# A transformer layer on one core: x in four transfers with spread column sums, row factors spread by TensorE, a late modulation in small pieces, other buffers for w_out

## The chip, the cores and the metric

The kernel runs on one core of one Trainium2 chip. The metric is the device time of one execution in microseconds (us), lower is better. TensorE is called PE in the views of the profile, VectorE DVE, ScalarE ACT, GpSimd POOL, and SyncE SP; SP issues nearly all transfers. All arithmetic is in 32 bits.

## What is computed

One layer over 512 latent tokens with a context of 256 tokens, model width 1024. `w_ada` turns a condition vector into shifts, scales and gates; the first two of its six parts are needed at once, the other four (w_ada_b in the kernel) only for the output projection and the feed-forward part.

```python
mod = jax.nn.silu(c) @ w_ada[l] + b_ada[l]
sh1, sc1, g1, sh2, sc2, g2 = jnp.split(mod[:, None, :], 6, axis=-1)
a_lat = _modulate(x, norm_mix[l], sh1, sc1)       # rmsnorm * gain * (1 + scale) + shift
a_ctx = _modulate(xc, norm_mix[l], csh1, csc1)
# one projection of both by w_in: pooling input, q, k, v, o of 4 heads, two gates
#   pooling: window means over the 8 x 64 grid, a 256 x 256 product per group
#   mLSTM, 4 heads, forward and backward, chunks of 128 tokens:
S = einsum('bhtd,bhsd->bhts', qc, kc) * exp(Dm - m[..., None])
num = einsum('bhts,bhsv->bhtv', S, vc) + sa[..., None] * einsum('bhtd,bhdv->bhtv', qc, C0)
h = num / jnp.maximum(jnp.abs(den), jnp.exp(-m))[..., None]
y = sigmoid(p[5]) * pool_out + sigmoid(p[6]) * m_out
x = x + g1 * (y @ w_out)
x = x + g2 * _swiglu(_modulate(x, norm_ffn[l], sh2, sc2), w_ffn_in[l], w_ffn_out[l])
return _rmsnorm(x, norm_final)
```

## The kernel before

**Products.** Every product of two 32-bit operands is made of three matmuls on a high and a low part of each (`mm3`): high by high, high by low, low by high. Activations lie with channels on the partitions. Each weight block of 128 output channels (512 KB) comes through `wload`: SP issues its transfer into one of three buffers `wr`, ACT casts the high part (`wh`), DVE subtracts to give the low part (`wl`); both have two buffers. Other destinations are named by an argument: "wide" gives the two buffers gh and gl, ("oh", "ol") the five half-width buffers of each of these. Each engine works in program order; where the program is not ordered by hand (`manual_schedule`, used for the start and the feed-forward part's first tiles), a scheduler orders it.

**Start.** SP issues the parameters, x in eight transfers of 256 KB (one per block k of 128 channels), a tile of ones, an identity, then alternately `ada` (1 MB, one block of the first two parts of w_ada) and `wr` (w_in for six output tiles, block k). For the RMS of x, ACT squares each block, DVE adds the squares up into one tile, and PE takes column sums with a 128x2 tile of ones as the moving operand (`rstd_cols`); POOL takes the power -0.5, and PE spreads the result over the partitions (`rstd_rows`). PE multiplies zeros (`keep_warm`, tile `warm`) in between, in numbers given by `WARM`. `mod_rows` and `mod_cols` compute the shift and scale of block k, `stage` modulates block k, `products` multiplies it with six tiles of w_in.

**Heads.** For each of four heads: values, scores and applications in two halves of 256 query tokens (`scores(0)`, a filling projection tile, `apply(0)`, `scores(1)`, another tile, `turn`, `apply(1)`), then the pooling for two tiles, gates, and q and k of the next head. `decays` makes the exponential decay factors (tiles E) for a half: a row factor per query, which lies in 32 rows, is needed on all partitions. `gates` writes these 32 rows to memory (tile `rd`), and each `decays` reads its four rows back as a broadcast. POOL adds the masks, ACT takes the exponentials, DVE multiplies the scores, and the products are split into high and low parts Sp.

**Late modulation.** `late_mod` fetches 32 blocks of w_ada_b of 512 KB (tile `pb`, two buffers, shared with the pooling) and forms each product with the condition row and its sum in one DVE instruction. It is called after the keys of the next head, 11 blocks after each of heads 1 and 2, and 10 after head 3.

**Output projection.** Eight tiles of w_out; the first two run over the first six of eight input blocks, then over the other two. Tiles 2 and 3 use `wh` and `wl`, 4 and 5 gh and gl, 6 and 7 oh and ol. The feed-forward part follows.

## Time and profile before

| | before |
|---|---|
| device time, median of 3 runs | 902.11 us (901.39 to 903.74) |
| the profiled execution | 904.35 us, of which the span from first to last instruction is 902.6 us |
| PE busy | 880.6 us (98%) |
| DVE busy | 612.8 us (68%) |
| ACT busy | 434.0 us (48%) |
| POOL busy | 63.2 us (7%) |
| mean granted TensorE clock | 0.989 of 2.4 GHz |
| data moved | 121.20 MB, mean 134 GB/s |

1.75 us of the profiled execution lie outside its span. Busy shares are means over stages with different limits; matmuls are pipelined, so a busy PE is not one at its peak.

### The profile page before, as it was taken

How to read it: one execution, taken by the hardware profiler on the slowest of the kernel's cores; microseconds unless marked ns; L12 is line 12 of the kernel's file. 1: busy time of each engine (PE TensorE's matmuls, PEld its weight loads, DVE VectorE, ACT ScalarE, POOL GpSimd, SP SyncE). 2: the span in 40 equal slices, each digit the busy share in tenths (PEclk: the TensorE clock that was granted, in tenths of full speed). 3: DMA queues.
4: the chain of work that ended last, by engine and by line, in shares of the span. 5: the costliest groups of instructions: out<-in, count | busy, mean ns of one | idle time of the engine just before them, and what ended most of it. 6: DMA issues, size and time to landing. Idle time of an engine off the chain costs nothing.

```text
span 902.6 us, 14972 instructions
## 1 busy us (share of the span) xinstructions
PE 880.6 (98%) x5879; PEld 798.9 (89%) x5879; DVE 612.8 (68%) x1183; ACT 434.0 (48%) x822; POOL 63.2 (7%) x92
## 2 busy tenths in 40 slices
PE   7999999999999999999999899999999999999996
PEld 6679888899888998889988699999889998899996
DVE  3679656856599676886778658895366854867544
ACT  3455354555433552335543348574145741666442
POOL 0000010010000000001000000020011100111000
PEclk8999999999999999999999899999999999999998
DMA  9934031322067312662148750384366643766402
GB/s 338 323 105 152 9 90 33 128 83 82 24 202 253 90 51 82 220 225 82 48 152 270 245 180 29 86 216 120 94 160 147 150 117 88 204 141 129 130 1 94
DMA packets 42438, 121.20 MB, mean 134 GB/s; under 512 B 4577, under 2 KB 9345, under 8 KB 41345
## 3 DMA queue, kind: packets, MB, share of 16 engines
q1 hardware_dynamic: 36896, 110.29, 37.9%
q0 software_dynamic: 5472, 9.96, 6.7%
q8 instruction: 46, 0.75, 0.3%
q14 instruction: 24, 0.19, 0.1%
HBM read 116.55 MB, written 3.69 MB: 133 GB/s over the span
## 4 chain that ended last, share of the span: by engine, by line
PE 69%; DVE 12%; DMA 10%; issue 4%; ACT 3%; SPq 0%; POOL 0%; DVEq 0%; POOLq 0%; ACTq 0%
PE ps L181 14%; PE ps L183 14%; PE ps L182 14%; DMA pb<-in_wada_b 6%; DVE wl L152 3%; PE pat L327 3%; PE ps L540 2%; PE ps L541 2%; PE ps L539 2%; PE pat L745 2%; PE pat L743 2%; PE pat L744 2%; PE pat L182 2%; PE pat L181 2%; PE pat L183 2%
## 5 line engine op out<-in xcount | busy, mean ns | idle before, releaser
L151 ACT CAST wh<-wr 128x1024 fp32r<-128x1024 f32 (+3 forms) x80 | 80.8, 1011 | 120.7 <-PE ps L182 92.1
L181 PE MATMUL ps<-a,wh 128*128 128x512 f32 (+1 forms) x368 | 138.8, 377 | 0.0
L182 PE MATMUL ps<-a,wh 128*128 128x512 f32 (+1 forms) x368 | 138.5, 376 | 0.0
L183 PE MATMUL ps<-a,wl 128*128 128x512 f32 (+1 forms) x368 | 138.4, 376 | 0.0
L152 DVE TENSOR_TENSOR wl<-wr,wh 128x1024 fp32r<-128x1024 f32 (+3 forms) x80 | 94.2, 1179 | 36.7 <-ACT wh L151 35.6
L183 PE MATMUL ps<-act,wl 128*128 128x512 f32 (+1 forms) x216 | 78.8, 365 | 3.0 <-DVE wl L152 3.0
L183 PEld LDWEIGHTS ps<-a,wl 128*128 128x128 f32 x368 | 69.3, 188 | 12.8 <-DVE wl L152 0.2
L181 PEld LDWEIGHTS ps<-a,wh 128*128 128x128 f32 x368 | 69.3, 188 | 12.1
L182 PEld LDWEIGHTS ps<-a,wh 128*128 128x128 f32 x368 | 69.3, 188 | 11.8
L181 PE MATMUL ps<-act,wh 128*128 128x512 f32 (+1 forms) x216 | 78.4, 363 | 1.4 <-ACT wh L151 1.3
L182 PE MATMUL ps<-act,wh 128*128 128x512 f32 (+1 forms) x216 | 78.2, 362 | 0.0
L540 PE MATMUL ps<-wl,a 128*128 128x256 f32 (+1 forms) x192 | 54.4, 283 | 0.9 <-DVE wl L152 0.9
L539 PE MATMUL ps<-wh,a 128*128 128x256 f32 (+1 forms) x192 | 54.3, 283 | 0.0
L541 PE MATMUL ps<-wh,a 128*128 128x256 f32 (+1 forms) x192 | 54.2, 282 | 0.0
L972 POOL DMA_DIRECT2D ol<-in_wffi x38 | 33.4, 888 | 255.9 <-ACT ol L971 89.5
L181 PE MATMUL ps<-hp,gh 128*128 128x256 f32 x176 | 50.2, 285 | 1.0 <-ACT pat L1010 1.0
L1181 DVE SCALAR_TENSOR_TENSOR x<-ps,lb,x 128x512 f32<-128x512 f32 (+1 forms) x32 | 19.6, 616 | 45.3 <-PE ps L183 45.3
L183 PEld LDWEIGHTS ps<-act,wl 128*128 128x128 f32 x216 | 41.3, 191 | 10.2 <-DVE wl L152 4.3
L182 PE MATMUL ps<-hp,gh 128*128 128x256 f32 x176 | 49.0, 278 | 0.0
L183 PE MATMUL ps<-hp,gl 128*128 128x256 f32 x176 | 48.9, 278 | 0.0
L181 PEld LDWEIGHTS ps<-act,wh 128*128 128x128 f32 x216 | 41.4, 192 | 8.0 <-ACT wh L151 1.7
L182 PEld LDWEIGHTS ps<-act,wh 128*128 128x128 f32 x216 | 41.3, 191 | 6.5 <-DVE act L171 0.3
(309 smaller groups left out, 2541.5 us busy)
## 6 DMA issues: line engine op xcount, KB each, us to landing
wr<-in_w SPq DMA_DIRECT2D x42, 512.0 KB, 3.5
pb<-in_wada_b SPq DMA_DIRECT2D x32, 512.0 KB, 4.5
wr<-in_wffi SPq DMA_DIRECT2D x25, 512.0 KB, 4.4
ur<-in_wffi SPq DMA_DIRECT2D x19, 512.0 KB, 4.0
ol<-in_wffi POOLq DMA_DIRECT2D x38, 256.0 KB, 5.0
ada<-in_wada_a SPq DMA_DIRECT2D x8, 1024.0 KB, 8.1
wr<-in_wffo SPq DMA_DIRECT2D x16, 448.0 KB, 3.7
x<-in_xT SPq DMA_DIRECT2D x16, 256.0 KB, 6.0
```

Source lines behind the costliest of these rows:

```text
L151: nc.scalar.copy(wh, raw[:, :n])
L152: V.tensor_sub(wl, raw[:, :n], wh.bitcast(F32))
L181: nc.tensor.matmul(dst, wh, ah, start=first and i == 0, stop=False, skip_group_check=on)
L182: nc.tensor.matmul(dst, wh, al, start=False, stop=False, skip_group_check=on)
L183: nc.tensor.matmul(dst, wl, ah, start=False, stop=last and i == n - 1, skip_group_check=on)
L327: nc.tensor.matmul(acc0[i], w_first[k][i][w], aT[k][x], start=k + w + x == 0, stop=k == KT - 1 and w == 1)
L539: nc.tensor.matmul(acc[:, :n], ah, wh, start=kk == 0, stop=False)
L540: nc.tensor.matmul(acc[:, :n], ah, wl, start=False, stop=False)
L541: nc.tensor.matmul(acc[:, :n], al, wh, start=False, stop=kk == KT - 1)
L743: nc.tensor.matmul(o, sh_, vh[:, s, :], start=n == 0, stop=False)
L972: nc.gpsimd.dma_start(l, dram, accum_op=ALU.add)
L1181: V.scalar_tensor_tensor(x1[j][:, c], acc[:, c], g2[:, j:j + 1], x1[j][:, c], ALU.mult, ALU.add)
```

## The change

- x comes in four transfers of 512 KB, two blocks each; the ones are set by POOL and not fetched.
- The column sums of x are taken per pair of blocks: ACT squares one block, DVE the other and adds, and PE sums each pair at once, two sums and then a matmul of zeros. `WARM` is changed.
- In head 0, first half, the row factors are spread over the partitions by four matmuls with a broadcast column of the identity, and a DVE copy. The other seven `decays` read memory as before.
- `late_mod` hands out its blocks one or two at a time: two after the second application of head 0, and for each of heads 1 to 3 one after each of the six value tiles and two after each application.
- w_out tiles 2 and 3 go to gh and gl, 4 and 5 to oh and ol, 6 and 7 to wh and wl; the casts of 2 to 7 are held behind the last low part of y. In the feed-forward part the first pair of tiles goes to gh and gl, the second to oh and ol.

```diff
@@ -41,7 +42,7 @@
 NPAR = 168
 U0, Q0, K0, O0, G5, G6 = 0, 8, 16, 24, 32, 40
-WARM = (27, 2, 0, 1, 0)
+WARM = (16, 1, 2, 2, 5)
 NOSYNC = mybir.DependencyInfo(mybir.DependencyClass.NoSync, mybir.DependencyReason.DATA)
@@ -122,11 +123,13 @@
     V.tensor_scalar(quarter_mg, parm[:, C_MG:C_MG + KT], 0.25, None, ALU.mult)
-    x_sb = [tl("x", [P, T], F32, KT) for _ in range(KT)]
-    for k in range(KT):
-        nc.sync.dma_start(x_sb[k], xT[:, k * T:(k + 1) * T])
+    x_sb = []
+    for k in range(0, KT, 2):
+        xx = tl("x", [P, 2 * T], F32, KT // 2)
+        nc.sync.dma_start(xx, xT[:, k * T:(k + 2) * T])
+        x_sb += [xx[:, :T], xx[:, T:]]
     ones = small([P, P], "ones")
-    nc.sync.dma_start(ones, consts[:, P:2 * P])
+    nc.gpsimd.memset(ones, 1.0)
     ident = small([P, P], "ident")
@@ -190,15 +193,18 @@
+        q = None
+
         def __init__(self, urgent=()):
-            self.q = S("tmp")
             self.urgent = urgent
             self.n = {}
             self.last = {}
         def add(self, src, c):
             n = self.n[c.start] = self.n.get(c.start, 0) + 1
+            if self.q is None:
+                self.q = S("tmp")
             if n == 1:
@@ -219,6 +225,9 @@
                     nc.tensor.matmul(bank[:, 2 * i:2 * i + 2], q[:, o], ones[:, 0:2], start=t + i == 0,
                                      stop=t == len(terms) - 1, skip_group_check=True)
+            return self.power(bank, n)
+
+        def power(self, bank, n):
             sd = tl("rc", [P, 4], F32, 2)
@@ -242,9 +251,7 @@
     manual = tc.manual_schedule(engines={mybir.EngineType.PE, mybir.EngineType.Activation, mybir.EngineType.DVE})
     manual.__enter__()
-    stx = SumSq((0,))
-    for k in range(KT):
-        stx.add(x_sb[k], ALL)
+    stx = SumSq()
     rs_x = S("m")
@@ -327,8 +334,19 @@
     nf = len(FIRST)
-    sd = stx.rstd_cols(ALL)
-    keep_warm(WARM[1], warm)
+
+    bank = PS()
+    for k in range(0, KT, 2):
+        a, b = S("tmp"), S("tmp")
+        nc.scalar.activation(a, x_sb[k], AF.Square)
+        V.tensor_mul(b, x_sb[k + 1], x_sb[k + 1])
+        V.tensor_add(a, a, b)
+        for i in range(T // P):
+            nc.tensor.matmul(bank[:, 2 * i:2 * i + 2], a[:, i * P:(i + 1) * P], ones[:, 0:2], start=k + i == 0,
+                             stop=k == KT - 2, skip_group_check=True)
+            if i % 2 and k + i < KT - 2 + T // P - 1:
+                keep_warm(WARM[1], warm)
+    sd = stx.power(bank, T // P)
     rows = mod_rows(0)
@@ -491,12 +509,16 @@
             pass
-    def late_mod(lo, hi):
-        for i in range(lo, hi):
+    late = iter(range(16, 48))
+
+    def late_mod(n, behind):
+
+        for i in itertools.islice(late, n):
             wa = tl("pb", [P, PBW], F32, 2)
             nc.sync.dma_start(wa[:, :D], wada_b[i])
-            V.scalar_tensor_tensor(wa[:, :D], wa[:, :D], 0.5, crow_s, ALU.mult, ALU.mult,
-                                   accum_out=mods[:, i:i + 1])
+            with tc.issue_after(behind.ins):
+                V.scalar_tensor_tensor(wa[:, :D], wa[:, :D], 0.5, crow_s, ALU.mult, ALU.mult,
+                                       accum_out=mods[:, i:i + 1])
@@ -547,7 +569,9 @@
                     V.tensor_add(gif[:, :, d, j, :], gsrc[:, d], bsrc[:, d])
             nc.scalar.copy(vh[:, i, :DH], acc[:, :DH])
-            V.tensor_sub(vl[:, i, :DH], acc[:, :DH], vh[:, i, :DH].bitcast(F32))
+            low = V.tensor_sub(vl[:, i, :DH], acc[:, :DH], vh[:, i, :DH].bitcast(F32))
+            if h:
+                late_mod(1, low)
         return vh, vl
@@ -627,6 +651,13 @@
         rd = dram.tile([32, P], F32, name="rd")
         nc.sync.dma_start(rd, rows)
+
+        acc = PS("pat")
+        for k in range(4):
+            i = k // 2 * 16 + k % 2
+            nc.tensor.matmul(acc[:, k * P:(k + 1) * P], ident[:32, i:i + 1].broadcast_to([32, P]), rows, start=True, stop=True)
+        sa0 = S("E")
+        V.tensor_copy(sa0, acc)
         gx, c1, em = free[1:4]
@@ -645,15 +676,16 @@
                     nc.scalar.activation(wj[:, d, 0:j, :], wj[:, d, 0:j, :], AF.Exp)
                     V.tensor_scalar(wj[:, d, 0:j, :], wj[:, d, 0:j, :], 1.0 / 64.0, None, ALU.mult)
-        yield dict(g=g, gx=gx, m0=m0, c1=c1, em=em, ws=ws, rd=rd)
+        yield dict(g=g, gx=gx, m0=m0, c1=c1, em=em, ws=ws, rd=rd, sa0=sa0)
     def decays(h, gt, th):
-        sa, msk = S("E"), S("tmp")
-        nc.sync.dma_start(sa.rearrange("p (d j t) -> p d j t", d=2, j=2),
-                          gt["rd"].rearrange("(o d h j) t -> h o d j t", o=1, d=2, h=H)
-                          [h][:, :, 2 * th:2 * th + 2, :].broadcast_to([P, 2, 2, P]))
+        sa, msk = gt["sa0"] if h + th == 0 else S("E"), S("tmp")
+        if h + th:
+            nc.sync.dma_start(sa.rearrange("p (d j t) -> p d j t", d=2, j=2),
+                              gt["rd"].rearrange("(o d h j) t -> h o d j t", o=1, d=2, h=H)
+                              [h][:, :, 2 * th:2 * th + 2, :].broadcast_to([P, 2, 2, P]))
         for d, m in ((0, maskF), (1, maskB)):
@@ -760,7 +792,8 @@
             nc.gpsimd.tensor_tensor(rst[:, c2], ss[:, c2], mhalf[:, :2], ALU.pow)
             for t in range(2):
-                V.tensor_scalar(hs[t], hs[t], rst[:, 2 * th + t:2 * th + t + 1], None, ALU.mult)
+                done = V.tensor_scalar(hs[t], hs[t], rst[:, 2 * th + t:2 * th + t + 1], None, ALU.mult)
+            late_mod(2 if h or th else 0, done)
             return th, hs
@@ -842,7 +875,6 @@
         if h < H - 1:
             q_, k_ = queries(h + 1) if h else q1, keys(h + 1)
-        late_mod(16 + 11 * (h - 1), min(48, 16 + 11 * h)) if h else None
@@ -853,7 +885,9 @@
     for j in (6, 7):
-        ys[j] = tsplit(ylast[j - 6], "act")
+        ys[j] = S("act", F32R), S("act", F32R)
+        nc.scalar.copy(ys[j][0], ylast[j - 6])
+        ylow = V.tensor_sub(ys[j][1], ylast[j - 6], ys[j][0].bitcast(F32))
     close_pool("mix")
@@ -883,12 +917,15 @@
         accs.append((PS(), wload(wout[j], D)[0]))
         mm3(accs[j][0], accs[j][1][:6], ys[:6], last=False)
+    with tc.issue_after(ylow.ins):
+        w23 = [wload(wout[j], D, "wide")[0] for j in (2, 3)]
     for j, (acc, w) in enumerate(accs):
         mm3(acc, w[6:], ys[6:], first=False)
         proj_out(j, None, ALL, acc)
     for j in range(2, NW):
-        proj_out(j, wload(wout[j], D)[0], ALL)
-    wo = {j: wload(wout[j], D, "wide" if j < NW + 2 else ("oh", "ol"))[0] for j in range(NW, KT)}
+        proj_out(j, w23[j - 2], ALL)
+    with tc.issue_after(ylow.ins):
+        wo = {j: wload(wout[j], D, ("oh", "ol") if j < NW + 2 else None)[0] for j in range(NW, KT)}
@@ -1075,7 +1112,7 @@
     pw = []
     for j in range(2):
-        d = "wide" if j else None
+        d = ("oh", "ol") if j else "wide"
         pw.append((wload(wffi[2 * j], D, d)[0], wload(wffi[2 * j + 1], D, d)[0], act_tiles(j)))
```

The order in which engines meet these instructions moves at three places. First PE at the start of the program, from its first matmuls on (names: tmp_ are squares of x, summed; `ada` w_ada; rc the RMS factor). Before:

```order
L137 MATMUL pat_117<-warm 128x128 x27
L220 MATMUL ps_184<-ones,tmp_147 128x2 x4
L220 MATMUL ps_184<-ones,tmp_167 128x2 x4
L137 MATMUL pat_117<-warm 128x128 x2
L261 MATMUL ps_200<-ada_198,sil 32x256 x8
L233 MATMUL ps_211<-ident,rc_193 128x128 x4
L270 MATMUL ps_216<-ident,tmp_209 128x128 x2
L137 MATMUL pat_117<-warm 128x128
L261 MATMUL ps_238<-ada_236,sil 32x256 x8
```

With the change, from the last of x's third pair on:

```order
L345 MATMUL ps_142<-ones,tmp_165 128x2 x2
L140 MATMUL pat_109<-warm 128x128
L345 MATMUL ps_142<-ones,tmp_176 128x2 x2
L140 MATMUL pat_109<-warm 128x128
L345 MATMUL ps_142<-ones,tmp_176 128x2 x2
L268 MATMUL ps_191<-ada_189,sil 32x256 x8
L140 MATMUL pat_109<-warm 128x128 x2
L242 MATMUL ps_204<-ident,rc_186 128x128 x4
L277 MATMUL ps_209<-ident,tmp_200 128x128 x2
L140 MATMUL pat_109<-warm 128x128 x2
L268 MATMUL ps_232<-ada_230,sil 32x256 x8
L140 MATMUL pat_109<-warm 128x128 x5
```

The eight sums stood behind one block of zeros and are now in four groups, each pair of sums followed by zeros; zeros now also stand on both sides of the second `ada` group.

Second, DVE in head 1, between the scaling of the first application and the second application (Sp are low parts of decayed scores, wl a low weight part, tmp and E the factors). Before:

```order
L171 TENSOR_TENSOR Sp_2481<-tmp_2477,Sp_2480 128x512
L720 SCALAR_TENSOR_TENSOR tmp_2484<-pat_2464,g_ws,E_2327 128x256
L720 SCALAR_TENSOR_TENSOR tmp_2504<-pat_2491,g_ws,E_2327 128x256 x2
L171 TENSOR_TENSOR Sp_2488<-tmp_2484,Sp_2487 128x512
L712 SCALAR_TENSOR_TENSOR E_2332<-pat_2511,E_2332 128x256
L171 TENSOR_TENSOR Sp_2508<-tmp_2504,Sp_2507 128x512
L712 SCALAR_TENSOR_TENSOR E_2332<-pat_2511,E_2332 128x128
L712 SCALAR_TENSOR_TENSOR E_2338<-pat_2511,E_2338 128x128
L712 SCALAR_TENSOR_TENSOR E_2338<-pat_2511,E_2338 128x256
L171 TENSOR_TENSOR Sp_2527<-E_2332,Sp_2526 128x384
L171 TENSOR_TENSOR Sp_2533<-E_2338,Sp_2532 128x384
L152 TENSOR_TENSOR wl_2718<-wr_2715,wh_2717 128x1024
```

With the change:

```order
L520 SCALAR_TENSOR_TENSOR pb_2493,mods<-pb_2493,crow_s 128x1024
L520 SCALAR_TENSOR_TENSOR pb_2496,mods<-pb_2496,crow_s 128x1024
L174 TENSOR_TENSOR Sp_2516<-tmp_2512,Sp_2515 128x512
L752 SCALAR_TENSOR_TENSOR tmp_2519<-pat_2499,g_ws,E_2356 128x256
L752 SCALAR_TENSOR_TENSOR tmp_2539<-pat_2526,g_ws,E_2356 128x256 x2
L174 TENSOR_TENSOR Sp_2523<-tmp_2519,Sp_2522 128x512
L744 SCALAR_TENSOR_TENSOR E_2361<-pat_2546,E_2361 128x256
L174 TENSOR_TENSOR Sp_2543<-tmp_2539,Sp_2542 128x512
L744 SCALAR_TENSOR_TENSOR E_2361<-pat_2546,E_2361 128x128
L744 SCALAR_TENSOR_TENSOR E_2367<-pat_2546,E_2367 128x128
L744 SCALAR_TENSOR_TENSOR E_2367<-pat_2546,E_2367 128x256
L155 TENSOR_TENSOR wl_2759<-wr_2756,wh_2758 128x1024
```

Two late products now stand ahead of the first Sp of the second half, and wl, which came behind the last two Sp, now stands ahead of them.

Third, SP's queue of transfers ahead of the output projection. Before:

```order
L148 DMA wr_5306<-in_wout 128x1024
L497 DMA pb_5243<-in_wada_b 128x1024
L497 DMA pb_5246<-in_wada_b 128x1024
L148 DMA wr_5331<-in_wout 128x1024
L497 DMA pb_5249<-in_wada_b 128x1024
L148 DMA wr_5377<-in_wout 128x1024
L497 DMA pb_5252<-in_wada_b 128x1024
L497 DMA pb_5255<-in_wada_b 128x1024
L148 DMA wr_5415<-in_wout 128x1024
L497 DMA pb_5258<-in_wada_b 128x1024
L497 DMA pb_5261<-in_wada_b 128x1024
L148 DMA wr_5453<-in_wout 128x1024
```

With the change:

```order
L151 DMA wr_5310<-in_wout 128x1024
L151 DMA wr_5335<-in_wout 128x1024
L151 DMA wr_5359<-in_wout 128x1024
L151 DMA wr_5365<-in_wout 128x1024
L151 DMA wr_5458<-in_wout 128x1024
L904 DMA x_924_5293<-in_xT 128x512
```

The transfers of w_ada_b that stood between those of w_out are gone from here; they now stand in the heads.

## Rows read from the trace of the kernel before

**Rows 1.** The page's first part: busy time of each engine, its share of the span and its number of instructions.
```profile
PE 880.6 (98%) x5879; PEld 798.9 (89%) x5879; DVE 612.8 (68%) x1183; ACT 434.0 (48%) x822; POOL 63.2 (7%) x92
```

**Rows 2.** What TensorE (PE) waited for, over the whole span: waiting line, the releasing engine, tile and line, and then the us in total, the times and the longest.
```profile
PE ps L183 <- DVE wl L152: 3.0, 3, 2.1
PE ps L220 <- DVE tmp L210: 2.6, 1, 2.6
...
PE ps L181 <- ACT wh L151: 1.3, 1, 1.3
...
PE ps L327 <- ACT a L282: 1.0, 1, 1.0
PE pat L743 <- ACT Sp L170: 1.0, 1, 1.0
...
PE ps L540 <- DVE wl L152: 0.9, 1, 0.9
```

**Rows 3.** Busy time by stretch. Columns: the stretch, its length, then the busy us of each engine with its instructions, the granted TensorE clock as a share of 2.4 GHz, the DMA engines' mean busy share, GB/s. The stretches are the first 20 us; in head 0 the filling tile ahead of the first application and that application; the same two in head 2; the first 96 matmuls of the output projection, and a part of these.
```profile
0.00:20.00 20.00, 16.06 (x98) 14.37 (x99) 5.41 (x17) 7.64 (x12) 1.80 (x6) 0.83 0.89 330
118.18:124.16 5.98, 5.60 (x26) 4.35 (x25) 2.62 (x8) 3.79 (x12) 2.28 (x4) 1.00 0.42 142
124.16:133.33 9.17, 7.37 (x54) 6.76 (x55) 7.38 (x18) 6.86 (x18) 0.58 (x1) 1.00 0.20 29
314.78:320.23 5.45, 5.45 (x26) 4.51 (x25) 4.71 (x12) 3.99 (x11) 0.00 (x0) 1.00 0.40 117
320.23:326.69 6.46, 6.46 (x55) 6.45 (x54) 3.63 (x13) 3.79 (x10) 0.00 (x0) 1.00 0.37 98
493.32:522.07 28.75, 25.39 (x98) 19.76 (x96) 20.71 (x32) 11.96 (x19) 0.00 (x0) 0.88 0.81 264
515.20:521.98 6.78, 6.78 (x31) 5.58 (x30) 4.10 (x7) 3.75 (x7) 0.00 (x0) 1.00 1.01 378
```

**Rows 4.** The timeline of the first 24 us: start, length (of the whole run of instructions of one kind, with their count behind x), engine, line, operation, tiles, and in brackets the engine's idle time ahead of it and what ended that.
```profile
1.36 8.53 PE L137 MATMUL pat<-warm 128*128 128x128 f32 x54 [1.36 <-DVE warm L110]
...
9.34 3.08 DVE L210 TENSOR_TENSOR tmp<-tmp,tmp 128x512 f32<-128x512 f32 x4 [2.10 <-ACT tmp L206]
...
12.48 3.20 PE L220 MATMUL ps<-ones,tmp 128*128 128x2 f32 x16 [2.58 <-DVE tmp L210]
...
15.96 1.01 POOL L225 TENSOR_TENSOR rc<-rc,mhalf 128x4 f32<-128x4 f32 x1 [14.63 <-DVE rc L223]
...
16.67 1.94 PE L261 MATMUL ps<-ada,sil 128*32 128x256 f32 x16
...
18.53 1.72 PE L233 MATMUL ps<-ident,rc 128*128 128x128 f32 x8
...
20.09 0.38 PE L270 MATMUL ps<-ident,tmp 128*128 128x128 f32 x2
...
20.63 1.07 PE L261 MATMUL ps<-ada,sil 128*32 128x256 f32 x16
...
21.18 0.75 DVE L281 SCALAR_TENSOR_TENSOR tmp<-x,sm,ps 128x512 f32<-128x512 f32 x1
...
21.96 0.72 ACT L282 ACTIVATE a<-tmp,shm 128x512 fp32r<-128x512 f32 x1 [2.19 <-DVE tmp L281]
...
22.73 0.73 PE L327 MATMUL ps<-a,wh 128*128 128x512 f32 x2 [1.03 <-ACT a L282]
```

**Rows 5.** The chain of waits of the first 26 us, the last transfer of x: start (its issue), length, what.
```profile
4.49 6.76 DMA x<-in_xT
```

**Rows 6.** The transfers issued between 6 and 8.5 us, of them the first block of w_ada: issuing queue, count, KB each, us from issue to landing.
```profile
ada<-in_wada_a SPq DMA_DIRECT2D x1, 1024.0 KB, 7.9
```

**Rows 7.** The chain of waits between 111 and 134 us (head 0), in order of time: start, length, what.
```profile
112.39 2.07 DMA rd<-tmp
114.51 5.32 DMA E<-rd
119.99 0.75 POOL tmp L658
```

**Rows 8.** VectorE's timeline around the second application of head 1, columns as in Rows 4.
```profile
228.07 0.62 DVE L763 TENSOR_SCALAR tmp<-tmp,rst 128x256 f32<-128x256 f32 x2 [0.43 <-POOL rst L761]
...
232.78 1.09 DVE L171 TENSOR_TENSOR Sp<-E,Sp 128x384 fp32r<-128x384 f32 x2
235.15 1.23 DVE L152 TENSOR_TENSOR wl<-wr,wh 128x1024 fp32r<-128x1024 f32 x1 [1.27 <-ACT wh L151]
```

**Rows 9.** The instructions that touch the tile pb, which holds the late blocks of w_ada: duration in ns as min/median/max with the first and last start; and the transfers' us from issue to landing.
```profile
L498 DVE SCALAR_TENSOR_TENSOR pb<-pb,crow_s x32: 1205/1224/1227, 262.5 to 506.1; 128x1024 f32<-128x1024 f32 x32
...
DMA to landing us min/median/max: 3.4/4.5/5.7
```

**Rows 10.** The chain of waits between 495 and 515 us (output projection), columns as in Rows 7.
```profile
497.80 6.02 DMA wr<-in_wout
...
503.83 1.06 ACT gh L170
...
507.43 1.24 DVE wl L152
...
508.70 0.80 PE ps L183
509.50 0.43 PE ps L181
```

More of the change, by code (lines that the diff above doesn't have):

```diff
@@ L1 @@
+import itertools
 import math
```

## The prediction, made before the changed kernel ran

> **What bounds the kernel now.** I read the page's busy line first: PE is busy 880.6 of 902.6 us, the next engine, DVE, 68% [rows 1]. So PE sets the time, and a change that takes no matmul away can gain only where PE stands still, or runs at half its clock. The second view is the list of PE's waits [rows 2]. The named waits that this change can touch are 3.0 us for low weight parts (longest 2.1), 2.6 for the squares of x, 1.3 for a cast weight, 1.0 for the first modulated tile, 1.0 for a cast score product in head 0, 0.9 in the values. The reader is to see that they are few and that each belongs to one place. The third view, busy time by stretch, shows what the waits cost with their consequences [rows 3]: in the first 20 us PE is busy 16.06 at 0.83 of the clock; the filling tile and first application of head 0 take 5.98 + 9.17 us and those of head 2, with the same work, 5.45 + 6.46; the first 96 matmuls of the output projection take 28.75 us at clock 0.88, where a part of them at full clock shows 30 weight loads in 6.78 us, 0.226 us a matmul.
>
> **The start.** PE's chain to the first product at 22.73 is in the timeline [rows 4]: zeros until 9.9, 2.58 us idle for the squares, then 16 records of sums in 3.20 us, the first ada group 1.94, the spreading 1.72, transposes 0.38, after which DVE's modulation starts at 21.18 and ACT's part at 21.96. The sums, ada and the spreading ran at half clock: the second ada group at 20.63, same work at full clock, took 1.07 instead of 1.94. Now with the change. The last transfer of x landed at 4.49 + 6.76 = 11.25 [rows 5], the first ada block, issued at about 6.2, 7.9 us after issue, at 14.1 [rows 6]. The bytes in the queue ahead are the same but for the ones, so I leave both (14.0 for ada). Each pair costs DVE a square and an addition in a row, 2 x 0.77 (3.08 for four additions, [rows 4]); with the last two pairs close together the last sum tile is there at about 13.1. Its four sums with a zero matmul are ten records, about 0.1 each at full clock: 14.1. DVE's scaling and POOL's power (1.01) end at 15.4. PE meanwhile does the ada group, 14.1 to 15.2, two zero matmuls to 15.6, the spreading at full clock 0.86 to 16.5, transposes to 16.9. From the transposes' end to DVE's modulation it took 21.18 - 20.47 = 0.7, then 0.78 to ACT, then 0.77 to the product: 19.1. But five zero matmuls now stand ahead of the product, and behind the second ada group, which can't start before its block lands: 1 MB behind 0.4 MB of weights, at the 378 GB/s of the last stretch of [rows 3] 3.7 us after the first, 17.7. So 17.7 + 1.07 + ten records at 0.12 = 20.0. The gain is 22.73 - 20.0 = 2.7. Later stages hold PE longer (18 products and an ada group, 5 us and more) than their 3.7 us of transfer, so I pass the gain on whole. Bounds: if the clock falls all the same, the four groups cost 2.4 us more, gain 0.5; if x lands 2 us earlier by fewer transfers, 4.9.
>
> The Trainium skill, "DMA: Bandwidth & Descriptors", section "Rules for kernel authors", asks for transfers of at least 1 MiB, and its section "Anatomy of one DMA" fits a fixed part of about 2.0 us to each (of those that GpSimd issues; these are SP's). If the fixed parts added up, eight transfers of 256 KB would take about 21 us and four of 512 KB 13, an estimate from that page, and the start would gain some 8 us. The trace differs: all eight landed within 10.1 us of the first issue [rows 5], so the fixed parts overlap.
>
> **Head 0.** The rows of factors go to memory in 2.07 us and come back in 5.32, and only at 119.99 can POOL add masks [rows 7]; that is 7.4 us in which PE has just 4.2 us of scores and its filling tile to do. The loss is 15.15 - 11.91 = 3.2 us [rows 3]. With the change the rows reach the partitions by four matmuls and a DVE copy; POOL can start at about 114.2, and ACT's exponentials are done before the old ones began. The second half still reads memory, and its first exponential stands on ACT ahead of three casts for the first half; the transfer lands at about 119.9 as before, which leaves those casts some 3 us. The four matmuls are unseen before; by the spreading at the start, the nearest, 1.72 at half clock or 0.86 at full; by the transposes 2 x 0.38. I take 0.8. Gain 2.4, bounds 0 and 2.9.
>
> **The output projection.** The chain reads [rows 10]: a w_out transfer issued at 497.80, its cast to gh at 503.83 ahead of the next cast on ACT, DVE's low part at 507.43, PE at 508.70, and then 0.43 us a matmul for about 6 us. SP's queue shows why the loads came late: between two w_out loads stood one or two of w_ada_b, each waiting for a pb buffer that DVE had to free. With the change those blocks are spread over the heads, the w_out loads wait only for wr buffers, and tiles 2 and 3 have buffers of their own, so their parts are ready by about 500, and PE needs them from 504. The loss is 28.75 - 96 x 0.226 = 7.0 us, of which 3.4 are named waits and the rest the half clock. I take all 7.0; bound below 3.5, if another cast stalls once for 1 to 2 us and the clock falls again. In the values of head 3 the 0.9 us for late low weights [rows 2] belongs to the same queue and goes too. The moved buffers of the feed-forward part change casts from one of 1024 to two of 512 columns, two loads, hidden beside PE's products there: nothing, at most 0.6.
>
> **Late products.** The 32 products still cost DVE 1.22 us each [rows 9], but now inside the heads, where DVE's order matters. In the values each stands behind a low part, and its transfer is issued only when the product two before it is done; with 3.4 to 5.7 us to landing, median 4.5, and value tiles ending every 1.4 to 2.9 us, the last three wait for data, and what is queued behind them is the low part of the next value tile and then the scaling of the first scores. I work out that these start 1.2 us late at 3.7 us to landing, which the filling tile covers, and 2.7 late at 4.5, when PE waits about 1.3. Off the old crowded stretch I take near the short end: 0.3 a head, bounds 0 and 1.5. After the first application of heads 1 to 3 two products, 2.5 us, stand between 228.69 and the first Sp, and a low weight part that waits for its cast until 235.15 now stands ahead of the last two Sp, which were done at 233.87 [rows 8]. They come at about 236.9, PE wants them from 236.1: 0.7 a head, bounds 0 and 2.4. The pairs behind the second applications and in head 0 meet only pooling work, cover enough. Together 3 x (0.3 + 0.7) = 3.0.
>
> **Sum.** 2.7 + 2.4 + 7.0 + 0.9 - 3.0 = 10.0 us. The profiled execution took 904.35, 1.75 of it outside the span; it becomes 894.35. It stood 2.24 above the median, so on the median's scale 892.1. About 0.3% (2.7 us) is what a measurement of this kernel can tell from no change.
>
> **The rivals.**
> - *DVE's queue costs much more.* Each product waits its 4.5 us, 1.5 a value stage and 2.4 a second application for three heads, 11.7 instead of 3.0: 900.8; cases from 897. For it: DVE stood idle for pb before. Against: before, 11 came in a row beside the next head's weights.
> - *Slower than before.* PE waits for the last Sp of the second application in heads 1 to 3 for 2.6 us, long enough that, as at 508.70, it then runs at half clock for some 6 us, 3.2 more each: 17.4 us instead of 3.0, 906.5. It decides from 16 us together. The trace has the wait of 2.1 us with this consequence, but no such wait in a head. The Trainium skill, "TensorE: Matmul & The Clock Gate", "Architectural detail", says that ACT and DVE are strict FIFO, which lets nothing pass a waiting product; the ACT cast at 503.83 that held up the one behind it and DVE's low part behind it agree [rows 10].
> - *The start gains nothing*, since the clock falls with the sums' few columns, or ada's landing sets it: 894.3.
> - *The output projection keeps half its stall* in another cast: 895.6.
> - *x lands 2 us earlier*, the fixed parts having mattered: 889.9.
>
> **How the numbers follow.** Chances: forecast 0.55 (own range 888.5 to 895.5), DVE's queue 0.14, slower 0.05, start nothing 0.12, half a stall 0.08, x early 0.06. Bounds at their best give 904.35 - 15.7 - 2.24 = 886.4 (4.9 + 2.9 + 7.0 + 0.9, no loss). The range 886.5 to 898.5 leaves out the slower case, the worse half of DVE's queue and a little below. Faster than 899.4: all but that half and the slower case, 0.88; same 0.07; slower 0.05.
>
> **What would show it.** In the changed profile: the first product of the start near 20 us and no half clock from 12.9 to 19.8; in head 0 filling tile and application in about 12 us; the first 96 matmuls of w_out in about 21.8 us at full clock; no PE wait for a low weight part there; and new PE waits for Sp or score factors of about 1 us in each of heads 1 to 3. The forecast fails if these waits reach 2 us and pull the clock down, or if the stretch of w_out still shows 0.43 us a matmul.

## The result, and the profile after

The changed kernel takes 890.24 us in the median of four runs (889.56 to 892.23) against 902.14 for the kernel before beside it: ratio 0.9869, 95% interval 0.9848 to 0.989. In a later series it took 891.94 against 902.8, 0.9885 (0.9853 to 0.9917). The trace of the changed kernel is that of the slowest of the four runs, 892.23 us, span 890.5.

Page, first part, changed kernel:

```profile
PE 877.3 (99%) x5907; PEld 798.2 (90%) x5907; DVE 614.3 (69%) x1188; ACT 432.8 (49%) x820; POOL 66.0 (7%) x93
```

PE's waits in the changed kernel, columns as in [rows 2]:

```profile
PE pat L242 <- POOL rc L234: 1.1, 1, 1.1
PE ps L184 <- ACT pat L1047: 1.0, 1, 1.0
PE ps L186 <- DVE wl L155: 0.9, 2, 0.5
...
PE ps L345 <- DVE tmp L343: 0.6, 1, 0.6
```

The wait for cast score products, that in the values and those of the output projection are gone. What they cost with their consequences is in the stretches, columns as in [rows 3]; here four of the start, then head 0's filling tile and first application, head 1's second application, and the first 96 matmuls of the output projection:

```profile
8.00:10.00 2.00, 2.00 (x20) 2.00 (x19) 1.79 (x4) 0.63 (x1) 0.00 (x0) 1.00 1.05 397
10.00:12.00 2.00, 1.92 (x17) 1.73 (x16) 1.63 (x3) 0.63 (x1) 0.00 (x0) 1.00 0.99 411
12.00:14.00 2.00, 2.00 (x10) 2.00 (x10) 0.00 (x0) 0.00 (x0) 0.00 (x0) 0.52 1.05 443
...
18.00:20.00 2.00, 2.00 (x19) 1.75 (x22) 0.68 (x4) 0.00 (x0) 0.00 (x0) 0.78 1.02 365
118.38:123.82 5.44, 5.44 (x26) 4.51 (x25) 4.28 (x10) 3.61 (x9) 1.44 (x2) 1.00 0.06 20
123.82:130.28 6.46, 6.46 (x55) 6.45 (x54) 4.77 (x13) 4.29 (x10) 0.00 (x0) 1.00 0.45 131
231.45:238.33 6.88, 6.86 (x57) 6.64 (x56) 5.17 (x17) 3.70 (x9) 0.00 (x0) 1.00 0.29 88
490.05:511.81 21.76, 21.76 (x97) 18.02 (x96) 14.76 (x20) 10.80 (x17) 0.00 (x0) 1.00 0.80 273
```

Against [rows 3]: 11.90 instead of 15.15 in head 0, and 21.76 instead of 28.75 at full clock in the output projection. In the start PE is busy from 7.6 us on, after 0.6 us of waiting for the first sum tile (the last line of the waits), and yet the clock falls at 12.1 us, and is back at 18.9.

Because the program runs the same matmuls, PE's matmuls that begin and end a stage can be set side by side in all traces. This table, worked out from their start times, carries most of what follows (us; "before" has the traces of three executions):

| stage | before | changed | changed again | undo_start | undo_spread | undo_late | undo_wout | late_after_scores |
|---|---|---|---|---|---|---|---|---|
| to the first product | 22.73, 24.05, 21.94 | 21.72 | 19.79 | 19.61 | 19.55 | 21.62 | 19.88 | 18.32 |
| on to head 0's scores | 91.21, 91.18, 91.16 | 92.42 | 92.39 | 92.47 | 91.16 | 92.42 | 92.42 | 92.42 |
| head 0: scores, filling tile, application | 19.40, 21.98, 21.97 | 16.14 | 16.02 | 16.02 | 21.86 | 16.02 | 16.02 | 16.02 |
| second applications, heads 1 to 3 | 19.73, 19.68, 19.68 | 20.66 | 20.94 | 20.67 | 20.90 | 19.73 | 20.91 | 19.73 |
| from head 2 to head 3's scores | 81.66, 81.49, 82.34 | 80.44 | 80.42 | 80.41 | 80.41 | 81.66 | 80.42 | 80.39 |
| first 96 matmuls of w_out | 28.75, 28.47, 28.09 | 21.76 | 21.76 | 21.76 | 21.76 | 22.75 | 22.50 | 21.76 |
| on to the feed-forward's 256-column products | 23.91, 23.91, 23.91 | 23.91 | 23.91 | 23.91 | 23.91 | 24.67 | 23.91 | 23.91 |
| from there to the last matmul | 350.00, 350.86, 348.68 | 347.63 | 350.91 | 351.17 | 349.87 | 350.17 | 351.36 | 349.13 |

In the first pair of traces the spans differ by 12.1 us: start -1.0, spreading +1.2, head 0 -3.3, second applications +0.9, values of head 3 -1.2, w_out -7.0, feed-forward part -2.4, and +0.7 in small pieces. *zeros3*, *zeros0* and *eight_x*, below, differ from the changed kernel at the start only; in all three head 0 takes 16.02 and w_out 21.76 too, and the second applications take 20.8 to 21.1.

### The profile page after: what moved, and what is told of

Same layout as the page of the kernel before. It is cut to its first block, busy times and chain, and to the rows that moved or that the text cites. A ratio compares the mean times of both kernels' runs of the same rounds, so it can differ in the third digit from the quotient of the medians.

```text
span 890.5 us, 15009 instructions
## 1 busy us (share of the span) xinstructions
PE 877.3 (99%) x5907; PEld 798.2 (90%) x5907; DVE 614.3 (69%) x1188; ACT 432.8 (49%) x820; POOL 66.0 (7%) x93
## 4 chain that ended last, share of the span: by engine, by line
PE 88%; DVE 5%; DMA 2%; ACT 2%; issue 2%; SPq 0%; DVEq 0%; POOLq 0%; POOL 0%; ACTq 0%
PE ps L184 20%; PE ps L186 19%; PE ps L185 19%; PE pat L334 3%; PE ps L561 3%; PE ps L563 3%; PE ps L562 3%; PE pat L777 2%; PE pat L775 2%; PE pat L776 2%; PE pat L185 2%; PE pat L184 2%; PE pat L186 2%; DMA wr<-in_wffo 1%; PE ps L334 1%
## 5 line engine op out<-in xcount | busy, mean ns | idle before, releaser
L154 ACT CAST wh<-wr 128x1024 fp32r<-128x1024 f32 (+3 forms) x78 | 78.8, 1011 | 115.5 <-PE ps L185 89.4
L155 DVE TENSOR_TENSOR wl<-wr,wh 128x1024 fp32r<-128x1024 f32 (+3 forms) x78 | 91.7, 1176 | 44.3 <-ACT wh L154 42.9
L1218 DVE SCALAR_TENSOR_TENSOR x<-ps,lb,x 128x512 f32<-128x512 f32 (+1 forms) x32 | 19.6, 616 | 45.2 <-PE ps L186 45.2
L184 PE MATMUL ps<-hp,oh 128*128 128x256 f32 x176 | 48.8, 277 | 0.1
L185 PE MATMUL ps<-hp,oh 128*128 128x256 f32 x176 | 48.6, 276 | 0.0
L186 PE MATMUL ps<-hp,ol 128*128 128x256 f32 x176 | 48.4, 276 | 0.0
```

Source lines behind the costliest of these rows:

```text
L154: nc.scalar.copy(wh, raw[:, :n])
L155: V.tensor_sub(wl, raw[:, :n], wh.bitcast(F32))
L184: nc.tensor.matmul(dst, wh, ah, start=first and i == 0, stop=False, skip_group_check=on)
L185: nc.tensor.matmul(dst, wh, al, start=False, stop=False, skip_group_check=on)
L186: nc.tensor.matmul(dst, wl, ah, start=False, stop=last and i == n - 1, skip_group_check=on)
L1218: V.scalar_tensor_tensor(x1[j][:, c], acc[:, c], g2[:, j:j + 1], x1[j][:, c], ALU.mult, ALU.add)
```

## The experiments

**Undoing one part each.** The four kernels below are the changed one with one part as before; the diffs are those hunks of the change, reversed. They ran together, with the kernel before at 903.8 us (899.45 to 909.07) and without the changed kernel. Their ratios stand against 0.9869 and 0.9885 of the changed kernel, and the intervals of all but undo_spread overlap both of its intervals; so a cost read from the medians is good to some 3 us, and the stages of the table price the parts better.

*undo_start*: x, ones, sums and `WARM` as before.

> The changed kernel with the start of before (x in eight transfers, ones fetched, sums behind one block of zeros, the old numbers of zeros); everything else as changed. Theory: the start is worth what its own stretch shows. In the profiled execution of the changed kernel the first product came at 21.72 instead of 22.73, with TensorE at half clock from about 12 to 19 us; the mean clocks of its other executions (0.995 to 0.996 against 0.992) say that the clock did not fall there, which gives some 2.3 us more. So undoing costs 1.0 us where the clock falls, about 3.3 where it does not: median 892.5 to 893.5 against 890.2. Rival: the start is bounded by the transfers of w_ada in any case, and undoing costs under 0.5 us.

894.63 us, above the 892.5 to 893.5 expected; ratio 0.9903 (0.9868 to 0.9938). The trace gave the first product at 19.61, earlier than four of the six traces of the changed start here; it also had half clock for only some 3 us. One trace can't price the start; see the repeats below.

*undo_spread*: the row factors read from memory (the hunk of `decays`; the four matmuls and the copy go too).

```diff
-        sa, msk = gt["sa0"] if h + th == 0 else S("E"), S("tmp")
-        if h + th:
+        sa, msk = S("E"), S("tmp")
```

> The changed kernel with head 0's first row factors read back from memory as before. Theory: the wait of the filling tile and the first application comes back (15.15 us for both instead of 11.90) and four matmuls, which took about 1.3 us, go: plus 2.0 us, median 892.2. Rival: the late products or the second half's read hid part of it, and the cost is under 1 us.

897.7 us, 0.9931 (0.9907 to 0.9954), the dearest of the four, and 5.5 above the median expected. Head 0 took 21.86 instead of 16.02 us, the four matmuls gave 1.26 back: 4.6 instead of 2.0. One part of the difference is in its chain of waits (start, length, what):

```profile
109.14 3.94 DMA rd<-tmp
113.14 5.01 DMA E<-rd
118.17 0.04 POOLq L682
118.31 0.75 POOL tmp L682
```

The way out to memory took 3.94 us here, 2.07 in [rows 7]. The other part is the clock: the application ran at half clock for some 3.4 us, which cost half of that. In the first trace of the kernel before, the clock held there [rows 3]; here:

```profile
122.47:132.58 10.11, 8.85 (x54) 8.23 (x55) 7.12 (x20) 7.46 (x20) 0.00 (x0) 0.83 0.12 30
```

*undo_late*: three bunches behind the keys again (one line of the diff; the calls in the values and behind the applications go).

```diff
+        late_mod(16 + 11 * (h - 1), min(48, 16 + 11 * h)) if h else None
```

> The changed kernel with the late modulation in three bunches behind the keys as before, and the changed buffers of w_out. Theory: it is the place of the w_ada_b transfers, between the w_out loads in SP's queue, that made the output projection late; the stall of about 7 us comes back at least by half, and the wait of 0.9 us in the values of head 3, while the 0.3 us at each second application of heads 1 to 3 goes: plus 3.5 to 7 us, median 894 to 897. Rival: the buffers alone cure the output projection; then undoing the placing costs 0 to 1 us.

895.58 us, 0.9902 (0.9867 to 0.9937): inside the 894 to 897 of the theory, but not for its reason. In the trace the wait in the values of head 3 is back (81.66), the second applications are as before (19.73), but w_out takes 22.75, only 1.0 more, and 0.8 goes into the projection's second part. The chain shows transfers of w_ada_b late in SP's queue again, and PE's clock holds all the same; the last line is the stretch of w_out:

```profile
497.01 4.41 DMA pb<-in_wada_b
501.42 0.02 issue
501.44 1.25 DVE pb L516 x2
502.69 0.02 issue
502.70 3.63 DMA x<-in_xT
...
489.93:512.68 22.75, 22.09 (x97) 17.94 (x96) 18.17 (x30) 8.12 (x15) 0.00 (x0) 1.00 0.82 268
```

*undo_wout*: the old buffers, small late pieces. The casts of tiles 2 to 7 are not held behind y either, so "buffers" stands here for buffers and order together.

> The changed kernel with the buffers of w_out and of the first feed-forward tiles as before, and the late modulation in small pieces. Theory: with the w_ada_b transfers out of the way the loads come early and the old buffers do with little wait: plus 0 to 1.5 us, median 890.2 to 891.7. Rival: the buffers are what counts, plus 4 to 7 us. Beside it: in the feed-forward part the changed kernel's 256-column matmuls followed each other every 113 ns in stretches where those of before took 118, 2.7 us together. If that comes from the buffers' places, it goes here; if it does not depend on them, it may be seen in any of the four kernels.

894.84 us, 0.9901 (0.9865 to 0.9936), beyond the 890.2 to 891.7 of the theory; w_out 22.50, 0.7 more than with the changed buffers, and no other stage above the spread of the other traces. So either edit alone takes away about six of the 7 us in the first 96 matmuls; the buffers alone leave 1.0 there and 0.8 in the second part, the small pieces alone 0.7. My theory, that the transfers' place decides, and its rival, that the buffers do, were both half right: the long stall needed late loads and the old buffers at once. With either edit the clock held as well, here in undo_wout's stretch:

```profile
488.31:510.81 22.50, 22.10 (x97) 17.94 (x96) 14.17 (x20) 11.60 (x18) 0.00 (x0) 1.00 0.81 270
```

In the kernel before, its fall made about half of the 7.0 us in the first trace (some 6.8 us at half clock, which cost about half of that), and about a quarter in the other two (some 3.4 us at half clock).

**Repeats, and the start.** The changed kernel, late_after_scores, zeros3 and a second trace of before ran together; zeros0, eight_x and a third trace of before ran later, beside a kernel before of 903.05.

> The changed kernel once more, for a second trace beside the others of this call. Theory: two things of the first trace are chance of the execution and not of the edit. At the start TensorE's clock falls in every kernel tried so far, but for 2 to 7 us, and the first product comes between 19.6 and 21.7 with the same program: here again in that range. In the feed-forward part the stretch from its first 256-column product to the last one took 347.6 us with the changed kernel, and 349.9 to 351.4 in kernels that have the same instructions there: here 349 to 351.5. Rival: both are the changed kernel's own, and come out as 21.7 and 347.6 again. The rest of the stages as in the first trace within 0.1 us: filling tile and first application of head 0 in 11.9, second applications of heads 1 to 3 in 6.9, the first 96 matmuls of w_out in 21.8.

891.94 us. First product 19.79, feed-forward stretch 350.91, w_out 21.76: the theory of chance holds for both. One stage left its 0.1 us: the second application of head 3 took 7.17 instead of 6.9. This execution has a mean clock of 0.995, and its clock did fall at the start, for some 3.4 us; so the mean clocks that undo_start's expectation went by don't tell whether the clock fell there.

> The kernel before once more, for a second trace. Theory: its start is as good as that of the changed kernel where the clock falls as briefly (with its start the otherwise changed kernel had the first product at 19.6): first product between 19.6 and 22.7; head 0's filling tile and first application 15 us or more, the 96 matmuls of w_out 28 to 29 us, the values' wait in head 3 there. Rival: the old start is slower by its own work, first product at 22 or later again. The feed-forward stretch: 350 to 351.5 by the theory of chance; the rival has no number for it.

908.46 us, a single run. First product at 24.05, outside the range expected and in that of the rival; feed-forward stretch 350.86, as expected. Head 0 took 21.98: the way through memory was little longer than in [rows 7], 2.23 and 5.74 us, but the clock fell in the application, 0.69 of full in the mean. The last line is the stretch of w_out:

```profile
10.00:12.00 2.00, 0.00 (x0) 0.00 (x0) 1.79 (x3) 1.83 (x4) 0.00 (x0) 0.82 1.02 411
12.00:14.00 2.00, 0.98 (x5) 0.98 (x5) 0.86 (x2) 0.52 (x1) 0.00 (x0) 0.50 1.03 422
...
126.03:137.21 11.18, 9.88 (x54) 9.29 (x55) 7.75 (x20) 7.46 (x20) 0.60 (x1) 0.69 0.19 29
496.83:525.29 28.46, 24.07 (x97) 18.86 (x96) 19.26 (x30) 10.44 (x17) 0.00 (x0) 0.94 0.78 261
```

> The kernel before a third time, for its start and its head 0. Theory: the old start lies on average some 2 us above the new one (22.7, 24.1, 19.6 so far, against 18.3 to 21.7), for TensorE stands idle 1.2 to 3.9 us for the last squares and the clock then falls: first product 21 to 24. Rival: the old start is as good as the new one, under 20.5. Head 0's filling tile and first application 14 us or more, 96 matmuls of w_out 28 to 29.

904.54 us, a single run: first product 21.94, head 0 21.97, w_out 28.09. Its application of head 0 and its w_out:

```profile
123.63:135.07 11.44, 9.76 (x54) 9.26 (x55) 7.69 (x20) 7.46 (x20) 0.54 (x1) 0.70 0.29 29
495.48:523.57 28.09, 24.14 (x97) 18.86 (x96) 19.39 (x30) 10.62 (x18) 0.00 (x0) 0.94 0.79 265
```

With undo_start's the old start gave 19.6 to 24.1, mean 22.1 of four traces; the changed start 18.3 to 21.7, mean 20.1 of six (its edit is in undo_spread, undo_late, undo_wout, late_after_scores and both traces of the changed kernel). That is some 2 us, from ranges that overlap. Most of it is the clock. Where it ran at half for some 3.4 us, the old start gave 19.61 and the changed one 19.55 to 19.88; for some 6.8 us, 21.94 and 22.73 against 21.62 and 21.72. The rest of the difference is one old trace with half clock for 10.2 us (24.05) and one changed trace without any (18.32). At equal clock the new start gains nothing to 1.1 us; whether it also keeps the clock up more often, ten traces can't tell.

*zeros3* and *zeros0* change only the number of zero matmuls between two pairs of sums, 1 in the change; the line is that of zeros3, zeros0 has 0 in that place:

```diff
-WARM = (16, 1, 2, 2, 5)
+WARM = (16, 3, 2, 2, 5)
```

> The changed kernel with three matmuls of zeros between each two column sums instead of one. In the changed kernel TensorE was busy from 7.6 to 12 us without a gap, and its clock fell to half all the same. Theory: sums with two columns and few zeros between are not enough work to hold the clock; with more zeros it stays at full to the first product, the ada group takes 1.07 instead of 1.66 to 1.94 and the spreading 0.9 instead of 1.6 to 1.9, but the sums end 0.5 to 1 us later; first product at 19 to 20. Rival: the clock does not depend on these zeros and falls as before.

> The changed kernel with no matmuls of zeros between the column sums of x. With one between two sums TensorE's clock fell to half at about 12 us in six of seven traces, with three it stayed. Theory: with none it falls as early or earlier, while the sums' 32 records end sooner, for the zeros took 0.24 us each pair of sums, 1.6 us in all where the sums were back to back; first product at 19 to 22. Rival: the zeros change nothing and only cost time; the clock falls for as long as with one, and the first product comes some 1 us earlier.

zeros3, 896.72 us, a single run, kept the full clock:

```profile
12.00:14.00 2.00, 2.00 (x19) 2.00 (x20) 0.00 (x0) 0.00 (x0) 0.00 (x0) 1.00 1.05 440
14.00:16.00 2.00, 2.00 (x24) 1.88 (x27) 0.16 (x1) 0.00 (x0) 0.04 (x1) 1.00 1.04 424
```

but its ada group began only at 15.61, and the first product came at 20.94, later than expected: the zeros stood in line ahead of the sums, which PE alone paced. Against the trace of one zero that kept its clock (18.32), they cost 2.6 us. zeros0, 893.89 us, a single run, lost the clock at 9.9 us, two us earlier than any trace with one zero, and had its first product at 20.41:

```profile
8.00:10.00 2.00, 1.50 (x13) 1.33 (x12) 1.90 (x4) 0.66 (x2) 0.00 (x0) 0.98 1.04 391
10.00:12.00 2.00, 1.87 (x9) 1.87 (x9) 1.37 (x3) 0.60 (x1) 0.00 (x0) 0.50 1.00 415
```

So zeros cost PE's own time. That they buy clock fits both traces but is not shown by one trace each, since with one zero the clock held in one execution too. Both first products lie within the 18.3 to 21.7 of one zero, so these traces don't rank the three. (The "six of seven" in zeros0's text counts undo_start, which has the old start; with one zero it was five of six by then, between 12.1 and 13.3 us, and eight_x below adds a sixth fall, at 12.3.)

*eight_x*: x in eight transfers, the sums by pairs.

```diff
-    for k in range(0, KT, 2):
-        xx = tl("x", [P, 2 * T], F32, KT // 2)
-        nc.sync.dma_start(xx, xT[:, k * T:(k + 2) * T])
-        x_sb += [xx[:, :T], xx[:, T:]]
+    x_sb = [tl("x", [P, T], F32, KT) for _ in range(KT)]
+    for k in range(KT):
+        nc.sync.dma_start(x_sb[k], xT[:, k * T:(k + 1) * T])
```

> The changed kernel with x in eight transfers of 256 KB again; the sums by pairs stay. Theory: the bytes set the time, not the number of transfers: the first square starts earlier (4.3 to 4.6 us instead of 5.7 to 6.0), the last pair's square between 9.3 and 10.5 as with four transfers, first product in the same 18.3 to 21.7. Rival: the fixed parts of eight transfers delay the last pair by 1 us or more, and the first product comes after 21.7.

894.71 us, a single run; first product 22.21, half a microsecond beyond the range. From its timeline, DVE's squares of the first, second and last pair:

```profile
5.05 0.69 DVE L340 TENSOR_TENSOR tmp<-x 128x512 f32<-128x512 f32 x1 [1.83 <-DMA x<-in_xT]
...
8.20 0.69 DVE L340 TENSOR_TENSOR tmp<-x 128x512 f32<-128x512 f32 x1 [1.67 <-DMA x<-in_xT]
...
11.00 0.69 DVE L340 TENSOR_TENSOR tmp<-x 128x512 f32<-128x512 f32 x1
```

The second pair came at 8.20, where four transfers had it at 6.9 to 7.4, and from there DVE's 1.4 us a pair carried the delay on: the last square stood at 11.00, outside the 9.3 to 10.5 expected. At the same half clock of some 6.8 us four transfers had the first product at 21.62 and 21.72, so eight cost 0.5 to 0.6 us there. One trace, so this is an indication.

**Late products behind the scores.** In heads 1 to 3 the first pair of late products moves behind the last low part of the second half's scores (`split` keeps its last subtraction in `lastlow`):

```diff
-            late_mod(2 if h or th else 0, done)
+            late_mod(2 if th else 0, done)
...
         p1 = scores(1, dec)
+        if h:
+            late_mod(2, lastlow[0])
```

> The changed kernel, but in heads 1 to 3 the two late products that stood between the first application's scaling and the second half's scores on DVE now stand behind the last low part of these scores. Theory: they were what made the second application of heads 1 to 3 0.3 us longer (6.88 to 6.89 against 6.57 to 6.61 before); now 6.55 to 6.61, minus 0.9 us in all, nothing lost elsewhere, since the weight part behind them is wanted some 5 us later. Rival: it was the weight part that moved ahead of the last two score parts, not the products; then it also goes, since the order is restored, but any stall would show at the tile behind the application instead.

889.17 us (887.62 to 890.83), ratio 0.9856 (0.9825 to 0.9888), beside the changed kernel's 891.94: the lowest median here, though the intervals overlap. The second applications are at 19.73 again, 0.9 to 1.2 us less, and none of the stages in the heads or the output projection grew. The rest of the 2.8 us is not this edit's as far as is known: against the second trace of the changed kernel, its trace has 1.5 us less in the start, whose program is the same, since the clock held there, and 1.8 us less in the feed-forward part, by chance (below). The start's stretch:

```profile
12.00:14.00 2.00, 2.00 (x28) 1.40 (x26) 0.16 (x1) 0.00 (x0) 0.67 (x1) 1.00 1.02 430
```

PE's timeline there shows the start at full clock, from the first ada group to the first product:

```profile
12.98 1.07 PE L270 MATMUL ps<-ada,sil 128*32 128x256 f32 x16
...
16.18 1.07 PE L270 MATMUL ps<-ada,sil 128*32 128x256 f32 x16
...
18.32 0.70 PE L336 MATMUL ps<-a,wh 128*128 128x512 f32 x2
```

## Why the prediction was right, and where its terms were off

The forecast of 892.1 us (886.5 to 898.5) held, and so did its sign. The sum was made of stalls with places, and most places behaved as named; the sizes of three terms were off. In the first pair the named terms measured 1.0 + 2.1 + 7.0 + 1.2 - 0.9 = 10.4 us, where the sum had 10.0: a start 1.7 too large and late products 2.1 too dear cancel. That the total came so close is in part luck.

- **The output projection**, 7.0 predicted, 7.0 in the first pair and 6.3 to 6.7 in the other traces of before. The step "96 matmuls at 0.226, the rest is stall and half clock" was right. What I did not see is that either half of the change would have done most of it. The split between wait and half clock was one trace's: in the other two the clock cost 1.7 us and not 3.4.
- **Values of head 3**, 0.9 predicted, 1.1 to 1.9: same queue, gone and back with undo_late.
- **Head 0**, 2.4 predicted. The four matmuls cost 1.2, not 0.8; the stall that they remove was 3.3 in the trace I had and 5.9 in two others. There the way through memory took 8.0 and 7.7 us instead of 7.4 and PE's idle time was the same, 2.2 to 2.4 us; what differs is that the clock ran at half for some 6.8 us, and not at all in the trace I had. So 2.1 there, 4.7 elsewhere. My estimate took one trace's stall for the kernel's.
- **The start**, 2.7 predicted, 1.0 in the first pair, some 2 as a mean. Two steps failed, in opposite ways. "I leave both (14.0 for ada)": the first ada block landed at 12.4 to 13.1 us in the traces with the changed start, and the one trace at full clock had its first product at 18.32, not 20.0. And "at full clock": some 6.8 us at half clock cost the changed start 3.4 us (21.7 against 18.3), where the bound had 2.4. That the mean of 20.1 meets the 20.0 is luck. (2.7 less 2.4 is 0.3, not the 0.5 of the bound, by which the rival's 894.3 goes.) I read the fall in [rows 4] as the consequence of 2.58 us of idle PE. In the changed kernel PE has no such idle ahead of the fall, and the timeline of the same matmuls shows the clock falling among the sums:

```profile
8.34 0.51 PE L345 MATMUL ps<-ones,tmp 128*128 128x2 f32 x4
...
11.99 0.96 PE L345 MATMUL ps<-ones,tmp 128*128 128x2 f32 x4
...
14.16 1.93 PE L268 MATMUL ps<-ada,sil 128*32 128x256 f32 x16
...
16.02 1.22 PE L140 MATMUL pat<-warm 128*128 128x128 f32 x4
...
21.72 0.71 PE L334 MATMUL ps<-a,wh 128*128 128x512 f32 x2
```

  The Trainium skill, "TensorE: Matmul & The Clock Gate", "Why this matters for your kernels", advises against idle gaps between bursts to keep the clock. Here the longest gap ahead of the fall was 0.6 us, and in the second trace of the changed kernel PE had no named wait at all between 3.66 and the fall at 13.1; a PE that was busy with sums of two columns and few zeros lost its clock, and the measurement decides.
- **The late products**, 3.0 predicted, 0.9 to 1.2 measured. In the values, where I took 0.3 a head, PE lost nothing in any trace: the transfers landed in 3.8 us in the median instead of 4.5, near the case of 3.7 that the filling tile was to cover. At the second applications I took 0.7 and found 0.3 to 0.6. The place was right: DVE's timeline in head 1 of the changed kernel has the two products, and the weight part ahead of the last two score parts:

```profile
225.60 1.22 DVE L520 SCALAR_TENSOR_TENSOR pb<-pb,crow_s 128x1024 f32<-128x1024 f32 x1
...
226.75 1.22 DVE L520 SCALAR_TENSOR_TENSOR pb<-pb,crow_s 128x1024 f32<-128x1024 f32 x1
...
232.15 1.22 DVE L155 TENSOR_TENSOR wl<-wr,wh 128x1024 fp32r<-128x1024 f32 x1
233.29 0.55 DVE L174 TENSOR_TENSOR Sp<-E,Sp 128x384 fp32r<-128x384 f32 x1
```

  The waits of about 1 us that were to show it are not in PE's list; the longest named one is 0.3, and the loss is in the stretch (6.88 us, PE busy 6.86). late_after_scores put both back and the loss went; which of the two made it stays open.
- **The feed-forward part** gave 2.4 us in the first pair that no step named. It is chance, below: the other traces with the changed instructions there take 349.1 to 352.5 us, those of before 348.7 to 350.9. The run that had it was the slowest of its four, so the median can't be put down to it.

Of the rivals, three did not come: PE did not pay for DVE's queue, nothing was slower, w_out kept no stall. "The start gains nothing" came half: the clock did fall among the sums, though that their few columns made it fall is not shown. "x lands 2 us earlier" came in part too: the last of x landed at 9.3 to 10.4 us in four transfers and at 9.9 to 11.8 in eight, about 1 us earlier in the mean.

## What to carry to other kernels

A stall on a nearly full TensorE is priced by its stretch, not by its named wait: a quarter to a half of what w_out lost was the clock that fell with the wait, and in head 0 nothing in one execution and more than half in two others. When two edits aim at one stall, undo each alone: here either one sufficed for five to six of seven microseconds. And a stall should be read from more than one trace, since the clock may fall in it or not: head 0 lost 3.3 us in one execution and 5.9 in the next. The same holds for a start: compare two of them at the same granted clock.

## What the runs showed of the hardware

Two things. First, the clock's fall among busy matmuls: with no zeros between the two-column sums it fell at 9.9 us (one trace), with one between 12.1 and 13.3 in six traces and not at all in a seventh, with three it stayed (one trace). The program of the start is the same in five of the six traces that fell and in the one that did not, so whether the clock falls, and for how long, differs between executions of one program.

Second, 256-column matmuls at full clock have two paces, about 113 and 118 ns, and stay in one for tens of microseconds. A pace is the time from one matmul's start to the next one's. Twenty microseconds of the feed-forward part, in this order the first trace of the changed kernel and its second, the same program and the same stretch:

```profile
811.74:831.74 20.00, 20.00 (x178) 19.95 (x177) 12.19 (x20) 12.57 (x23) 2.62 (x3) 1.00 0.50 117
```

```profile
811.74:831.74 20.00, 20.00 (x172) 20.00 (x172) 12.12 (x20) 11.49 (x21) 2.62 (x3) 1.00 0.51 118
```

PE is busy all the time in both, at full clock, with 178 and 172 matmuls. Over the whole part at full clock, 79% of the 256-column matmuls in the first trace are followed within 115.5 ns, and 28 to 61% in the other twelve traces. What sets it was not found; in the two traces of the changed kernel this part differs by 3.3 us, which is more than 0.3% of the whole.
